# Hybrid GLA and MLA decoder block: the mixer residual kept token-major, its gates summed across partitions by GpSimd

## The chip, the cores and the metric

One Trainium2 chip, one core of it. The metric is the device time of one execution in microseconds (us). The kernel before takes 1746.09 us, the median of three runs (1744.71 to 1747.65).

## What is computed

One decoder block on 256 tokens of width 2048 in float32. A token mixer runs two branches (gated linear attention and latent attention), merges them, projects the merge by `w_out` and adds it to the residual under a gate; a SwiGLU FFN of width 5632 follows. Six modulation vectors of length 2048 come from one product of the conditioning vector with `ada_w`, of which each is a 2048 x 2048 block.

```python
mod = (c_act @ ada_w[l] + ada_b[l]).reshape(B, N_MOD, D)[:, :, None, :]
shift_m, scale_m, gate_m, shift_f, scale_f, gate_f = [mod[:, i] for i in range(N_MOD)]
...
x = x + gate_m * token_mix(h, ...)          # token_mix ends in merged @ w_out
h = rmsnorm(x, norm_ffn_g[l]) * (1.0 + scale_f) + shift_f
x = x + gate_f * swiglu(h, ffn_w_in[l], ffn_w_down[l])
return rmsnorm(x, final_norm_g)
```

## The kernel before

**Weights.** Every weight is used once, for all 256 tokens, and is streamed from HBM in *halves*: 256 rows by 512 columns, 512 KB, one DMA each on SyncE's queue (`load_raw`, L96). A half lands in a tile of a ring (`raw_tile`, L87): six tiles of the pool `raw`, and where `more_raw` (L92) has lent a big slot, four more, which the profile names `s`. A load can start when the tile that it takes over, ten loads back in the program, has been read. `split_raw` (L101) then makes two float32r parts of the half: ScalarE casts the high part `hi` (L107), VectorE subtracts for the low part `lo` (L108). Three buffers of each let the split run up to three halves ahead of TensorE.

**Products.** Three matmuls per product of a tile (high by high, high by low, low by high). `form_a` (L160) keeps 128 tokens of the activation stationary and streams 512 weight columns: the result is token-major, two PSUM banks for the two token tiles. `form_b` (L170) keeps 128 weight columns stationary and streams the 256 tokens: the result is feature-major. A half is 12 matmuls of 512 columns in `form_a` and 24 of 256 in `form_b`. A *group* is 512 output columns: 8 halves for a depth of 2048.

**Modulation in the background.** `ada_steps(m, c0)` (L243) computes 512 columns of modulation vector m, a *strip*: eight loads of 512 KB through the same ring, and for each load two multiply-adds of VectorE by c into the tile `ada` (L265, L267). For m < 5 the strip's 128 partial sums per column are then turned by four TensorE transposes (L289) and summed along the free axis by ScalarE (L291), which gives the vector feature-major in `mod`. The strips stand in a list `bg`; `tick()` (L154) is called once per weight half and lets `background()` (L118) take a step or none, by a rate `pace[0]`. A step is one `yield` of the generator. The strips of m = 2, 4 and 3 (mixer gate, FFN scale and shift), twelve in all, start with the attention stage and are spread over it and the three 2048 x 2048 projections (`mla_wo`, `gla_wo`, `w_out`). At the start of `w_out`'s last group, `background(1000)` (L838) issues all that is left before that group's first half.

**Around the output projection** (L832 to L866). x, which the prologue has stored feature-major in DRAM (`x_sp`, L428), is fetched back in four parts into `x1`. Four groups of `form_b` on `w_out` follow; after each, VectorE adds gate times result to x (L846; the gate is a column of `mod`). ScalarE squares x1 (L853), VectorE adds the squares of the sixteen blocks, a few matmuls with ones sum over partitions (L858), `rsqrt_mean` (L191) finds the reciprocal norms in a chain of small VectorE operations, `rows_of` (L208) spreads them by a matmul, and `modulate` (L317) makes the FFN's input. In the FFN's first loop, eight `turn_x1` (L895) transpose x1 back to token-major, where the final sum needs it.

The order of instructions on each engine is fixed when the program is built, by a scheduler that moves what isn't pinned with `keep_in_program_order`.

Of the kernel before, what the change touches and what calls it, by code (L numbers as in the profile page):

```python
# [17 lines left out]
D = 2048  # L18
S = 256
# [32 lines left out]
def tile_block(ctx: ExitStack, tc: tile.TileContext, x, positions, ada_w, ada_b, w_in, gla_gk_w, gla_wo,  # L52
# [18 lines left out]
    def k256(t):  # L71
        return t.rearrange("p (k t) -> p k t", t=S)
# [86 lines left out]

    def form_a(ps, w, ah, al, k0, first, last, cols):  # L160
        for kk, (hi, lo) in enumerate(w):
            k = k0 + kk
            for t in range(2):
                ts = slice(t * P, (t + 1) * P)
                st, en = first and kk == 0, last and kk == len(w) - 1
                T.matmul(ps[t][:, :cols], lhsT=ah[:, k, ts], rhs=hi, start=st, stop=False)  # L166
                T.matmul(ps[t][:, :cols], lhsT=ah[:, k, ts], rhs=lo, start=False, stop=False)  # L167
                T.matmul(ps[t][:, :cols], lhsT=al[:, k, ts], rhs=hi, start=False, stop=en)  # L168
# [22 lines left out]
    def rsqrt_mean(dst, ssq, n, w, eng=None):  # L191
        v, l = sb(w, "rv"), sb(w, "rl")
        V.tensor_scalar(out=v, in0=ssq, scalar1=1.0 / n, scalar2=EPS, op0=ALU.mult, op1=ALU.add)
        yi = dst.bitcast(I32)
        V.tensor_scalar(out=yi, in0=v.bitcast(I32), scalar1=1, scalar2=None, op0=ALU.logical_shift_right)
        V.tensor_scalar(out=yi, in0=yi, scalar1=-1.0, scalar2=float(0x5F3759DF), op0=ALU.mult, op1=ALU.add)
        for _ in range(3):
# [45 lines left out]
    def ada_steps(m, c0, cols=512, quick=None):  # L243
# [36 lines left out]
        if quick is not None:  # L280
# [4 lines left out]
            V.tensor_tensor(out=mod[:, cs], in0=ps[:, :nb], in1=cb[:, cs], op=ALU.add)  # L285
        elif m < 5:
            ps = aux_bank()
# [37 lines left out]

    x_sp = dram.tile([P, 4096], F32, name="x_sp")
    ga_sp = dram.tile([P, 4096], F32, name="ga_sp")
# [98 lines left out]
    for r in range(4):  # L426
        if r == 3:
            tc.keep_in_program_order(nc.sync.dma_start(out=x_sp, in_=xT))  # L428
            more_raw(slot(5))
# [209 lines left out]
    def gla_att(h):  # L639
# [66 lines left out]
        atts[h] = attv  # L706

    for b in range(4):
        bg += [ada_steps(m, 512 * b) for m in (2, 4, 3)]
    pace[0] = 0.2  # L710
# [122 lines left out]
    x1 = slot(4)  # L833
    x1k = k256(x1)
    pace[0] = 0.6
    for i in range(4):
        if i == 3:
            background(1000)  # L838
        for n, ps in enumerate(group(form_b, w_out, 512 * i, k256(mh), k256(ml), KT)):
            tick()  # L840
            if n == 3:
                cs = slice(1024 * i, 1024 * (i + 1))
                tc.keep_in_program_order(nc.sync.dma_start(out=x1[:, cs], in_=x_sp[:, cs]))
        for j in range(4):
            k = 4 * i + j
            V.scalar_tensor_tensor(out=x1k[:, k], in0=ps[j // 2][:, (j % 2) * S:(j % 2 + 1) * S],  # L846
                                   scalar=mod[:, 32 + k:33 + k], in1=x1k[:, k], op0=ALU.mult, op1=ALU.add)

    acc = sb(512, "w0")[:, :S]
    ps = aux_bank()  # L850
    for k in range(KT):
        q = acc if k == 0 else sb(S, "e", 3)
        A.activation(out=q, in_=x1k[:, k], func=AF.Square)  # L853
        if 0 < k < KT - 4:
            V.tensor_tensor(out=acc, in0=acc, in1=q, op=ALU.add)
        if k >= KT - 5:
            for t in range(2):
                T.matmul(ps[:, t:t + 1], lhsT=(acc if k == KT - 5 else q)[:, t * P:(t + 1) * P], rhs=ones[:, 0:1],  # L858
                         start=k == KT - 5 and t == 0, stop=k == KT - 1, skip_group_check=True)
    rc2 = sb(2, "rx")  # L860
    rsqrt_mean(rc2, ps[:, 0:2], D, 2)
# [32 lines left out]

    def turn_x1(k):  # L895
        tp = aux_bank()
        for t in range(2):
            for kk in range(2):
                T.transpose(out=tp[:, t * S + kk * P:t * S + (kk + 1) * P],
                            in_=x1k[:, k + kk, t * P:(t + 1) * P], identity=ident)  # L900
        A.copy(out=x1tv[:, :, k * P:(k + 2) * P], in_=tp.rearrange("p (t d) -> p t d", t=2))
        yield

    assert not ATT.busy()
    for ch in range(FFN // 512):
# [107 lines left out]
```

## Time and profile before

| what | us |
|---|---|
| three runs | 1747.65, 1744.71, 1746.09 (median 1746.09) |
| the profiled execution | 1749.17 |
| span of its records | 1747.1 |
| TensorE busy | 1705.2 (98%) |
| VectorE, ScalarE, GpSimd busy | 1226.6, 847.6, 99.7 (70%, 49%, 6%) |

The profile is of one further execution, 3.1 us above the median. The span is what its records cover; 2.1 us lie around it. Matmuls overlap in the pipeline, so a matmul's pace is read from the distance of starts, not from its duration. The chain that ended last runs through TensorE, in short pieces of the last product. `w_out` runs from about 878 to 985 us, the FFN from 993 us.

### The profile page before, as it was taken

Reading aid. Unit: us, or ns where it says so; the run is one execution under the profiler, and the core shown is the slowest. Engines: PE = TensorE matmul, PEld = TensorE weight load, DVE = VectorE, ACT = ScalarE, POOL = GpSimd, SP = SyncE. Lnnn points to the kernel's source line nnn. Section 1 sums busy time; section 2 is a strip of 40 time slices with the busy share of each in tenths; the row PEclk is TensorE's granted clock in tenths of the full one; section 3 lists DMA queues with packets and bytes.
Section 4 is the critical chain, followed back from the end, with each engine's and each line's share of the span. In section 5 each row is a group of like instructions: output and inputs, shape, how many; then the busy total and the mean of one; then the engine's idle time right before and its main releaser. Section 6 shows DMA issues by size and latency. Waiting matters only on the chain. (4 is left out here: it accounts for less than half of the span.)

```text
span 1747.1 us, 24089 instructions
## 1 busy us (share of the span) xinstructions
PE 1705.2 (98%) x8888; PEld 1461.1 (84%) x8888; DVE 1226.6 (70%) x1764; ACT 847.6 (49%) x1300; POOL 99.7 (6%) x136
## 2 busy tenths in 40 slices
PE   6999999999999999999999899999999999999997
PEld 5898899889999887788899888888888888788885
DVE  6899987587787477988887856666664444555556
ACT  4644445355766655544444444444444444444443
POOL 1370000000000001000000000000000000000001
PEclk8999999999999999999999899999999999999998
DMA  9999897655455498999998678778776666555652
GB/s 353 323 325 314 300 302 226 182 188 170 144 151 180 123 313 259 343 372 349 336 323 297 212 206 272 242 232 277 240 232 191 182 191 190 178 189 191 192 191 99
DMA packets 207349, 418.47 MB, mean 240 GB/s; under 512 B 12960, under 2 KB 31840, under 8 KB 206592
## 3 DMA queue, kind: packets, MB, share of 16 engines
q1 hardware_dynamic: 205472, 410.39, 72.1%
q0 software_dynamic: 1616, 6.49, 1.0%
q8 instruction: 69, 1.13, 0.3%
q14 instruction: 48, 0.39, 0.1%
q10 hardware_dynamic: 144, 0.07, 0.0%
HBM read 408.51 MB, written 8.39 MB: 239 GB/s over the span
## 5 line engine op out<-in xcount | busy, mean ns | idle before, releaser
L108 DVE TENSOR_TENSOR lo<-raw,hi 128x1024 fp32r<-128x1024 f32 (+3 forms) x524 | 600.9, 1152 | 396.9 <-ACT hi L107 394.4
L107 ACT CAST hi<-raw 128x1024 fp32r<-128x1024 f32 (+3 forms) x524 | 512.4, 984 | 620.6 <-PE mm L168 391.1
L167 PE MATMUL mm<-lo,s 128*128 128x512 f32 (+1 forms) x1520 | 598.4, 394 | 2.6 <-DVE lo L108 2.6
L168 PE MATMUL mm<-hi,s 128*128 128x512 f32 (+1 forms) x1520 | 590.4, 390 | 1.7 <-DVE s L322 1.7
L166 PE MATMUL mm<-hi,s 128*128 128x512 f32 (+1 forms) x1520 | 543.2, 393 | 4.3 <-ACT hi L107 2.1
L166 PEld LDWEIGHTS mm<-hi,s 128*128 128x128 f32 x1520 | 286.7, 190 | 63.3 <-ACT s L321 3.1
L167 PEld LDWEIGHTS mm<-lo,s 128*128 128x128 f32 x1520 | 287.8, 189 | 61.4 <-DVE lo L108 5.2
L168 PEld LDWEIGHTS mm<-hi,s 128*128 128x128 f32 x1520 | 287.3, 189 | 58.7 <-DVE s L322 2.0
L267 DVE SCALAR_TENSOR_TENSOR ada<-raw,cact,ada 128x512 f32<-128x512 f32 (+1 forms) x293 | 211.1, 724 | 10.5 <-DMA raw<-in_ada_w_dram 7.6
L176 PE MATMUL mm<-s,hi 128*128 128x256 f32 x672 | 191.7, 286 | 0.0
L177 PE MATMUL mm<-s,hi 128*128 128x256 f32 x672 | 190.1, 284 | 0.0
L178 PE MATMUL mm<-s,lo 128*128 128x256 f32 x672 | 188.3, 284 | 0.0
L107 ACT CAST hi<-s 128x1024 fp32r<-128x1024 f32 (+1 forms) x76 | 78.2, 1029 | 106.5 <-PE mm L168 46.2
L176 PEld LDWEIGHTS mm<-s,hi 128*128 128x128 f32 x672 | 128.7, 192 | 0.8 <-issue 0.3
L177 PEld LDWEIGHTS mm<-s,hi 128*128 128x128 f32 x672 | 128.8, 192 | 0.4
L178 PEld LDWEIGHTS mm<-s,lo 128*128 128x128 f32 x672 | 127.5, 192 | 0.0
L108 DVE TENSOR_TENSOR lo<-s,hi 128x1024 fp32r<-128x1024 f32 (+1 forms) x76 | 91.7, 1207 | 27.1 <-ACT hi L107 26.5
L926 PE MATMUL mm<-lo,w 128*128 128x512 f32 x160 | 62.7, 392 | 0.0
L927 PE MATMUL mm<-hi,w 128*128 128x512 f32 x160 | 62.4, 392 | 0.0
L267 DVE SCALAR_TENSOR_TENSOR ada<-s,cact,ada 128x512 f32<-128x512 f32 (+1 forms) x79 | 57.7, 730 | 0.5
L925 PE MATMUL mm<-hi,w 128*128 128x512 f32 x160 | 50.5, 394 | 0.7 <-ACT w L933 0.7
L451 DVE TENSOR_TENSOR s<-mm,s 128x512 f32<-128x512 f32 (+1 forms) x62 | 40.1, 672 | 0.2
(270 smaller groups left out, 1594.1 us busy)
## 6 DMA issues: line engine op xcount, KB each, us to landing
raw<-in_ffn_w_in_dram SPq DMA_DIRECT2D x176, 512.0 KB, 4.4
raw<-in_ada_w_dram SPq DMA_DIRECT2D x150, 512.0 KB, 4.9
raw<-in_w_in_dram SPq DMA_DIRECT2D x128, 512.0 KB, 4.7
raw<-in_ffn_w_down_dram SPq DMA_DIRECT2D x88, 512.0 KB, 4.4
s<-in_ada_w_dram SPq DMA_DIRECT2D x42, 512.0 KB, 5.9
s<-in_w_in_dram SPq DMA_DIRECT2D x32, 512.0 KB, 4.7
raw<-in_mla_wo_dram SPq DMA_DIRECT2D x20, 512.0 KB, 6.5
raw<-in_gla_wo_dram SPq DMA_DIRECT2D x20, 512.0 KB, 6.9
```

What stands on the lines that cost most here:

```text
L107: A.copy(out=hh_, in_=rr)
L108: V.tensor_tensor(out=ll_, in0=rr, in1=hh_.bitcast(F32), op=ALU.subtract)
L166: T.matmul(ps[t][:, :cols], lhsT=ah[:, k, ts], rhs=hi, start=st, stop=False)
L167: T.matmul(ps[t][:, :cols], lhsT=ah[:, k, ts], rhs=lo, start=False, stop=False)
L168: T.matmul(ps[t][:, :cols], lhsT=al[:, k, ts], rhs=hi, start=False, stop=en)
L176: T.matmul(o, lhsT=hi[:, pick], rhs=ah[:, k], start=st, stop=False, skip_group_check=True)
L177: T.matmul(o, lhsT=hi[:, pick], rhs=al[:, k], start=False, stop=False, skip_group_check=True)
L178: T.matmul(o, lhsT=lo[:, pick], rhs=ah[:, k], start=False, stop=en, skip_group_check=True)
L267: ins = V.scalar_tensor_tensor(out=acc, in0=raw[:, k - k0], scalar=c, in1=acc, op0=ALU.mult, op1=ALU.add)
L925: T.matmul(o, lhsT=ah[:, ts], rhs=hi[:, ns], start=first, stop=False)
L926: T.matmul(o, lhsT=ah[:, ts], rhs=lo[:, ns], start=False, stop=False)
L927: T.matmul(o, lhsT=al[:, ts], rhs=hi[:, ns], start=False, stop=last)
```

## The change

1. `w_out` goes by `form_a`, in 384 matmuls of 512 columns instead of 768 of 256. In the last group the last two halves are kept until both are split, and the first token tile is finished before the second.
2. x1 is token-major. x is read from its input in four parts, and `x_sp` is gone. The gate is needed along the free axis, on all partitions: `gm` (slot 3) receives the bias of the gate by a broadcast DMA, and the gate's sums come from DRAM (`gm_sp`) by four broadcast DMAs. VectorE multiplies, adds, and ScalarE squares with a row sum (`accum_out`).
3. For m = 2, 3, 4 GpSimd's `partition_all_reduce` sums the strip's accumulator over partitions, into a second buffer of the two-buffer tag `ada`; then comes one more `yield`. For m = 2 a DMA on SyncE's queue writes the sums to `gm_sp`; for m = 3 and 4 VectorE picks the diagonal of the four 128 x 128 blocks into `mod`.
4. The strips of m = 2 come first, then 4 and 3 by turns.
5. x1 is transposed to feature-major (`x1T`, slot 0) ahead of `modulate`, 32 transposes; the 32 of `turn_x1` in the FFN are gone.
6. `rsqrt_mean` has one operation less.

```diff
-    def form_a(ps, w, ah, al, k0, first, last, cols):
+    def form_a(ps, w, ah, al, k0, first, last, cols, rows=(0, 1)):
...
-            for t in range(2):
+            for t in rows:
...
-        V.tensor_scalar(out=yi, in0=v.bitcast(I32), scalar1=1, scalar2=None, op0=ALU.logical_shift_right)
-        V.tensor_scalar(out=yi, in0=yi, scalar1=-1.0, scalar2=float(0x5F3759DF), op0=ALU.mult, op1=ALU.add)
+        V.tensor_scalar(out=yi, in0=v.bitcast(I32), scalar1=-0.5, scalar2=float(0x5F3759DF), op0=ALU.mult, op1=ALU.add)
...
-        elif m < 5:
+        elif m in (2, 3, 4):
+            ar = sb(512, "ada", 2)
+            G.partition_all_reduce(ar, acc, channels=P, reduce_op=bass_isa.ReduceOp.add)
+            yield
+            if m == 2:
+                tc.keep_in_program_order(nc.sync.dma_start(out=gm_sp[:, c0:c0 + cols], in_=ar[0:1]))
+                return
+            for i in range(nb):
+                d = ar[:, i * P:(i + 1) * P]
+                V.tensor_tensor_reduce(out=d, in0=d, in1=ident, scale=1.0, scalar=0.0, op0=ALU.mult, op1=ALU.add,
+                                       accum_out=mod[:, b0 + i:b0 + i + 1])
+            V.tensor_tensor(out=mod[:, cs], in0=mod[:, cs], in1=cb[:, cs], op=ALU.add)
+        elif m < 2:
...
-            tc.keep_in_program_order(nc.sync.dma_start(out=x_sp, in_=xT))
...
+    bg += [ada_steps(2, 512 * b) for b in range(4)]
     for b in range(4):
-        bg += [ada_steps(m, 512 * b) for m in (2, 4, 3)]
+        bg += [ada_steps(m, 512 * b) for m in (4, 3)]
...
+    def gate_mix(i, n):
+        cs = slice(512 * i, 512 * (i + 1))
+        if n == 0 and i == 0:
+            tc.keep_in_program_order(nc.sync.dma_start(out=gm, in_=ada_b[:, 2 * D:3 * D].to_broadcast([P, D])))
+        elif n == 1:
+            gr = sb(512, "sc", 2)
+            tc.keep_in_program_order(nc.sync.dma_start(out=gr, in_=gm_sp[:, cs].to_broadcast([P, 512])))
+            tc.keep_in_program_order(V.tensor_tensor(out=gm[:, cs], in0=gm[:, cs], in1=gr, op=ALU.add))
+        elif n == 3:
+            tc.keep_in_program_order(nc.sync.dma_start(
+                out=x1v[:, :, cs], in_=x[0, :, cs].rearrange("(t p) c -> p t c", p=P)))
+
     for i in range(4):
         if i == 3:
             background(1000)
...
+        for n in range(KT // 2):
+            w = half(w_out, 2 * n, 512 * i, 512)
+            if i == 3 and n >= 6:
+                kept.append((2 * n, w))
+            else:
+                form_a(ps, w, k256(mh), k256(ml), 2 * n, n == 0, n == 7, 512)
             tick()
...
+        for t in range(2):
+            for k, w in kept:
+                form_a(ps, w, k256(mh), k256(ml), k, False, k == KT - 2, 512, (t,))
+            u = sb(512, "sc", 2)
+            j = 2 * i + t
+            V.tensor_tensor(out=u, in0=ps[t], in1=gm[:, cs], op=ALU.mult)
+            V.tensor_tensor(out=x1v[:, t, cs], in0=x1v[:, t, cs], in1=u, op=ALU.add)
+            A.activation(out=u, in_=x1v[:, t, cs], func=AF.Square, accum_out=sq[:, j:j + 1])
+            if j in (3, 5):
+                V.tensor_tensor(out=sq[:, j - 1:j + 1], in0=sq[:, j - 1:j + 1], in1=sq[:, j - 3:j - 1], op=ALU.add)
...
-        if 2 <= ch < 10:
-            ATT.wait.append(turn_x1(2 * (ch - 2)))
```

**SyncE's queue ahead of `w_out`'s last group.** L98 is a load into the ring, `s_6858` and `s_6818` the lent slot's tiles. Before (L843 fetches a part of x):

```order
L98 DMA s_6858<-in_ada_w_dram 128x2x512
L98 DMA raw<-in_w_out_dram 128x2x512
L98 DMA s_6858<-in_w_out_dram 128x2x512
L98 DMA s_6858<-in_ada_w_dram 128x2x512 x2
L98 DMA raw<-in_ada_w_dram 128x2x512 x3
L98 DMA raw<-in_w_out_dram 128x2x512 x3
L98 DMA s_6858<-in_w_out_dram 128x2x512 x2
```

Now (L856 fetches a quarter of the gate's sums); the first row here is the third group's last half, the last row the fourth group's first two:

```order
L98 DMA raw<-in_w_out_dram 128x2x512
L98 DMA s_6818<-in_ada_w_dram 128x2x512
L98 DMA raw<-in_ada_w_dram 128x2x512
L856 DMA sc<-gm_sp 128x512
L98 DMA raw<-in_ada_w_dram 128x2x512 x3
L98 DMA s_6818<-in_ada_w_dram 128x2x512
L98 DMA raw<-in_ada_w_dram 128x2x512
L98 DMA s_6818<-in_ada_w_dram 128x2x512 x2
L98 DMA raw<-in_ada_w_dram 128x2x512
L98 DMA s_6818<-in_ada_w_dram 128x2x512
L98 DMA raw<-in_ada_w_dram 128x2x512 x5
L98 DMA s_6818<-in_w_out_dram 128x2x512 x2
```

Five loads of `ada_w` stood together there; sixteen stand there now, between the 24th and the 25th half of `w_out`.

**VectorE at the end of `w_out`'s third group.** Before, L846 is the gated add of that group, which needs its last matmul; the two splits (L108) ahead of it are the fourth group's first two halves:

```order
L267 SCALAR_TENSOR_TENSOR ada<-s_6858,cact,ada 128x512 x2
L108 TENSOR_TENSOR lo<-raw,hi 128x1024 x2
L846 SCALAR_TENSOR_TENSOR s_8370<-mm,mod,s_8370 128x256 x4
L267 SCALAR_TENSOR_TENSOR ada<-s_6858,cact,ada 128x512
L108 TENSOR_TENSOR lo<-raw,hi 128x1024
L855 TENSOR_TENSOR w_9464<-w_9464,e 128x256
L267 SCALAR_TENSOR_TENSOR ada<-s_6858,cact,ada 128x512
L855 TENSOR_TENSOR w_9464<-w_9464,e 128x256
L108 TENSOR_TENSOR lo<-s_6858,hi 128x1024
```

Now L881 is the multiplication by the gate, L882 the addition to x1 (`s_8283`; `s_8284` is the gate), L885 adds row sums, L266 is the multiply-add of the strips; the first row splits the third group's last half, the last row the fourth group's first:

```order
L108 TENSOR_TENSOR lo<-raw,hi 128x1024
L264 TENSOR_SCALAR ada<-s_6818,cact 128x512
L266 SCALAR_TENSOR_TENSOR ada<-s_6818,cact,ada 128x512
L881 TENSOR_TENSOR sc<-mm,s_8284 128x512 x2
L882 TENSOR_TENSOR s_8283<-s_8283,sc 128x512 x2
L885 TENSOR_TENSOR sq<-sq 128x2
L266 SCALAR_TENSOR_TENSOR ada<-raw,cact,ada 128x512 x10
L266 SCALAR_TENSOR_TENSOR ada<-s_6818,cact,ada 128x512 x4
L108 TENSOR_TENSOR lo<-s_6818,hi 128x1024
```

Fourteen multiply-adds have come to stand between the third group's end and the fourth group's first split; no split of the fourth group stands ahead of L881.

**GpSimd between attention and the output gate**, now (L287 is the all-reduce with the change of GpSimd's program ahead of it, L604 a store of branch gates, L198 to L201 the reciprocal norms of one GLA head; none of L287 stood here before):

```order
L604 DMA ga_sp<-raw 128x1024
L672 MEMSET s_3630 128x512
L287 ISA
L287 ISA ada<-ada 128x512
L604 DMA ga_sp<-raw 128x1024 x2
L198 ISA
L198 TENSOR_TENSOR rl<-gr 128x2
L199 TENSOR_TENSOR rl<-rl,rv 128x2
L200 TENSOR_SCALAR rl<-rl 128x2
L201 TENSOR_TENSOR gr<-gr,rl 128x2
```

The all-reduce has been put in ahead of two stores, and a change of program before and after it; three more such changes to the all-reduce follow later in the queue.

## Rows read from the trace of the kernel before

**Rows 1.** The page: busy us of each engine, share of the span, instructions.

```profile
PE 1705.2 (98%) x8888; PEld 1461.1 (84%) x8888; DVE 1226.6 (70%) x1764; ACT 847.6 (49%) x1300; POOL 99.7 (6%) x136
```

**Rows 2.** Windows: us, TensorE, its weight loads, VectorE, ScalarE, GpSimd, granted clock, DMA share, GB/s.

```profile
960.50:984.90 24.40, 24.40 (x207) 24.40 (x205) 20.25 (x31) 11.30 (x22) 1.15 (x2) 1.00 0.77 268
993.00:999.15 6.15, 6.14 (x15) 4.79 (x15) 6.15 (x17) 4.20 (x9) 0.00 (x0) 0.50 0.00 0
```

**Rows 3.** Timeline of TensorE, `form_b` on `w_out`: start us, us, line, operation; 24 matmuls apart.

```profile
958.23 0.28 PE L176 MATMUL mm<-s,hi 128*128 128x256 f32 x1
...
961.11 0.28 PE L176 MATMUL mm<-s,hi 128*128 128x256 f32 x1
```

**Rows 4.** Timeline of TensorE, `form_a` on `gla_wo`, 12 matmuls apart.

```profile
829.83 0.39 PE L167 MATMUL mm<-lo,s 128*128 128x512 f32 x1
...
832.55 0.39 PE L167 MATMUL mm<-lo,s 128*128 128x512 f32 x1
```

**Rows 5.** TensorE's transposes: timeline around four, the source view of line 289.

```profile
981.38 0.28 PE L177 MATMUL mm<-s,hi 128*128 128x256 f32 x1
...
982.06 0.28 PE L176 MATMUL mm<-s,hi 128*128 128x256 f32 x1
L289 PE MATMUL aux<-ident,ada x48: 271/272/273, 555.3 to 981.8; 128*128 128x128 f32 x48
```

**Rows 6.** Timeline of SyncE's DMA queue: start us, us, line, DMA, count.

```profile
940.04 2.03 SPq L98 DMA_DIRECT2D s<-in_ada_w_dram  x2
943.18 4.18 SPq L98 DMA_DIRECT2D raw<-in_ada_w_dram  x3
948.69 3.25 SPq L98 DMA_DIRECT2D raw<-in_w_out_dram  x3
```

**Rows 7.** Waits of SyncE's queue: waiter and releaser, us in all, times, longest.

```profile
SPq L98 <- DVE lo L108: 850.5, 430, 9.3
```

**Rows 8.** Timeline of VectorE: two multiply-adds, a split, two multiply-adds.

```profile
972.50 1.53 DVE L267 SCALAR_TENSOR_TENSOR ada<-raw,cact,ada 128x512 f32<-128x512 f32 x2
973.95 1.22 DVE L108 TENSOR_TENSOR lo<-s,hi 128x1024 fp32r<-128x1024 f32 x1
975.08 1.53 DVE L267 SCALAR_TENSOR_TENSOR ada<-raw,cact,ada 128x512 f32<-128x512 f32 x2
```

**Rows 9.** Groups by line and shape: count, busy us, mean ns, idle before.

```profile
L451 DVE TENSOR_TENSOR s<-mm,s 128x512 f32<-128x512 f32 x58 | 38.1, 682 | 0.1
L564 DVE CUSTOM_DVE_ANT_0 sc<-aux,cft 128x128 f32<-128x128 f32 x16 | 4.6, 287 | 11.4 <-PE aux L560 11.4
L107 ACT CAST hi<-raw 128x1024 fp32r<-128x1024 f32 x459 | 482.5, 1052 | 601.4 <-PE mm L168 378.5 <-PE aux L927 60.4 <-PE mm L177 50.8
L976 ACT ACTIVATE sc<-s 128x512 f32<-128x512 f32 x8 | 5.0, 630 | 15.8 <-DVE s L974 12.8 <-DVE rl L205 2.1 <-DVE rv L193 0.9
L976 ACT ACTIVATION_READ_ACCUMULATOR sc<-s 128x1 f32 x8 | 1.5, 186 | 0.0
```

**Rows 10.** DMA issues: count, KB each, median us from issue to landing.

```profile
raw<-in_ffn_w_in_dram SPq DMA_DIRECT2D x176, 512.0 KB, 4.4
```

**Rows 11.** Timeline of TensorE and VectorE between the output projection and the FFN.

```profile
984.46 0.28 PE L178 MATMUL mm<-s,lo 128*128 128x256 f32 x1
...
993.01 0.79 PE L166 MATMUL mm<-hi,s 128*128 128x512 f32 x1 [1.18 <-ACT s L321]
993.60 0.63 PE L167 MATMUL mm<-lo,s 128*128 128x512 f32 x1
994.03 0.63 PE L166 MATMUL mm<-hi,s 128*128 128x512 f32 x1
...
987.65 0.16 DVE L193 TENSOR_SCALAR rv<-aux 128x2 f32<-128x2 f32 x1 [0.65 <-PE aux L858]
```

**Rows 12.** GpSimd: the group of line 300, and line 300 by source.

```profile
L300 POOL PARTITION_ALL_REDUCE w<-ada x4 | 14.8, 3702 | 294.3 <-DVE ada L267 294.3
L300 POOLq MODIFY_POOL_CONFIG  x2: 33/35/37, 976.6 to 976.6; - x2
```

More of the change, by code (lines that the diff above doesn't have):

```diff
@@ L323, in modulate @@
                                op0=ALU.add, op1=ALU.subtract)
-    x_sp = dram.tile([P, 4096], F32, name="x_sp")
+    gm_sp = dram.tile([1, D], F32, name="gm_sp")
     ga_sp = dram.tile([P, 4096], F32, name="ga_sp")
@@ L833, in tile_block @@
     x1 = slot(4)
-    x1k = k256(x1)
+    x1v = x1.rearrange("p (t d) -> p t d", t=2)
+    gm = slot(3)[:, :D]
+    sq = sb(8, "sq")
     pace[0] = 0.6
+    def gate_mix(i, n):
[9 more added lines that the diff above has]
+                out=x1v[:, :, cs], in_=x[0, :, cs].rearrange("(t p) c -> p t c", p=P)))
     for i in range(4):
@@ L838, in tile_block @@
             background(1000)
-        for n, ps in enumerate(group(form_b, w_out, 512 * i, k256(mh), k256(ml), KT)):
-            tick()
[L841 to L856, printed above, removed]
+        ps = [mm_bank(), mm_bank()]
+        cs = slice(512 * i, 512 * (i + 1))
+        kept = []
+        for n in range(KT // 2):
[4 more added lines that the diff above has]
+                form_a(ps, w, k256(mh), k256(ml), 2 * n, n == 0, n == 7, 512)
+            tick()
+            gate_mix(i, n)
@@ new lines, in tile_block @@
+        for t in range(2):
[8 more added lines that the diff above has]
+                V.tensor_tensor(out=sq[:, j - 1:j + 1], in0=sq[:, j - 1:j + 1], in1=sq[:, j - 3:j - 1], op=ALU.add)
+            elif j == 7:
+                V.tensor_tensor(out=sq[:, 6:8], in0=sq[:, 6:8], in1=sq[:, 4:6], op=ALU.add)
@@ L857, in tile_block @@
+    assert not ATT.busy()
+    rc2 = sb(2, "rx")
+    rsqrt_mean(rc2, sq[:, 6:8], D, 2)
+    x1T = slot(0)
+    x1k = k256(x1T)
+    for k in range(0, KT, 2):
+        ps = aux_bank()
+        for kk in range(2):
             for t in range(2):
[L858 to L861, printed above, removed]
+                T.transpose(out=ps[:, kk * S + t * P:kk * S + (t + 1) * P],
+                            in_=x1v[:, t, (k + kk) * P:(k + kk + 1) * P], identity=ident)
+        A.copy(out=x1T[:, k * S:(k + 2) * S], in_=ps)
@@ L865, in tile_block @@
         modulate(k, x1k, r2, 3, k256(fh), k256(fl))
-    x1t = slot(0)
     more_raw()
-    x1tv = x1t.rearrange("p (t d) -> p t d", t=2)
     acts = [slot(3), slot(2), None]
@@ L893, in turn_act @@
             yield
[L895 to L902, printed above, removed]
     assert not ATT.busy()
@@ L958, in tile_block @@
             held.append((ah, al, ws))
-    ot = slot(4)
+    ot = slot(0)
     otv = ot.rearrange("p (t d) -> p t d", t=2)
@@ L970, in tile_block @@
             ns = slice(n * 512, (n + 1) * 512)
-            d = x1tv[:, t, ns]
+            d = x1v[:, t, ns]
             u = sb(512, "ada", 2)
@@ L983, in tile_block @@
             if n < 2:
-                A.activation(out=otv[:, t, ns], in_=x1tv[:, t, ns], func=AF.Copy, scale=fr)
+                A.activation(out=otv[:, t, ns], in_=x1v[:, t, ns], func=AF.Copy, scale=fr)
             else:
-                V.scalar_tensor_tensor(out=otv[:, t, ns], in0=x1tv[:, t, ns], scalar=fr, in1=fg[:, ns],
+                V.scalar_tensor_tensor(out=otv[:, t, ns], in0=x1v[:, t, ns], scalar=fr, in1=fg[:, ns],
                                        op0=ALU.mult, op1=ALU.mult)
```

## The prediction

> **What bounds the kernel now.** Read the page first: TensorE is busy for 1705 us, 98% of the span [rows 1], and the chain of waits that ended last runs through it. So a change counts by what it takes from TensorE's queue, and by what it makes TensorE wait. The windows come next: in the output projection's last group TensorE and its weight loads are busy in every one of the 24.4 us, VectorE in 20.3 of them, and the DMA engines for 77% [rows 2]. Nothing there waits, but nothing has much room. Third, the waits of SyncE's queue: for 850 us it stood at a ring tile that VectorE had still to split [rows 7]. The ring is always full; what stands ahead in that queue delays what stands behind.
>
> **The sum, part by part.** It is made against the profiled execution's own 1749.2 us; the median of the runs shown is 3.1 lower, and the forecast is given against the median.
>
> *Form of the product.* A half in `form_b` takes 961.11 - 958.23 = 2.88 us [rows 3], in `form_a` 832.55 - 829.83 = 2.72 [rows 4]. The 24 halves of the first three groups give 24 x 0.16 = **-4.0**. The fourth group is walked through below.
>
> *Transposes of the strips.* From the matmul before four of them to the second one after it are 982.06 - 981.38 = 0.68 us, where two steps of 0.12 would be 0.24: four cost 0.44 [rows 5]. The trace has 48 from 555 us on, twelve strips, one of them in the fourth group: 11 x 0.44 = **-4.8**. On ScalarE the twelve sums go too, on VectorE 32 diagonals come (0.29 us each [rows 9], and a short read of the sum); neither engine sets the pace there, so I count nothing. Were VectorE's cover gone, the 32 would cost some 10 us.
>
> *Transposes of x1.* The FFN loses 32: 8 x 0.44 = **-3.5**. They come back in fours ahead of the FFN: sixteen in groups that TensorE bounds, **+1.8**; eight fall into the wait below, eight into the gap before the FFN.
>
> *The fourth group.* This is where I expect the loss. The extra `yield` takes a step of the background's budget for every strip without loading anything, so about ten loads fewer are done by the start of the last group, and `background(1000)` then issues the rest at once. The order shows it: sixteen strip loads in SyncE's queue ahead of that group's first half, where there were five. In the trace the five were issued between 940 and 947 us, the next half of `w_out` at 948.7 [rows 6], and TensorE never noticed, since two splits of the fourth group stood ahead of the third group's end. Now none does. Walk it from T, TensorE's last matmul of the third group:
> - VectorE: two multiplications and two additions of 0.68 [rows 9], then the row-sum addition waits for ScalarE's last square (0.63, its read 0.19 [rows 9]): T + 3.9.
> - Fourteen multiply-adds at (973.95 - 972.50) / 2 = 0.725 [rows 8]. The twelfth, at T + 12.6, frees the ring tile into which the fourth group's first half goes. It lands 4.4 us later [rows 10], ScalarE casts it in 1.05 [rows 9]: TensorE starts at about T + 18.2. The second half follows by 2.
> - The third half's tile is freed only by the next strip's second multiply-add. That stands behind both splits (975.08 - 973.95 = 1.13 each [rows 8]), four diagonals and the gate's addition: T + 24; with landing and cast, T + 29.3. TensorE has by then finished two halves and stands again.
> - From there VectorE has six splits and nine multiply-adds, 6 x 1.13 + 9 x 0.725 = 13.3: T + 42.6. The last matmuls come some 3.9 later, T + 46.5.
>
> The same stretch took 24.4 [rows 2]: **+22.1**. [...]
>
> *From the last matmul to the FFN.* Before, the norm's first operation starts 987.65 - 984.46 = 3.2 us after the last matmul's start, 2.9 after its end [rows 11]. Now the order puts two splits of the FFN's halves among the last products: a split that ends some 0.85 after TensorE, a multiplication, an addition, the second split, an addition, ScalarE's square and its read, the row-sum addition: 0.85 + 0.68 + 0.68 + 1.13 + 0.68 + 0.83 + 0.2 = 5.1, less 0.2 for the operation that `rsqrt_mean` lost: **+2.0**. That operation is also gone from the chains at start and end: **-0.4**.
>
> *GpSimd and SyncE.* An all-reduce takes 3.7 us [rows 12]; GpSimd idles, but four writes of the gate's sums now stand in SyncE's queue and hold it until the sums exist. Bounds: nothing, if the all-reduce is over when the queue arrives, and 4 x 3.7 = 14.8 if the queue is always there first. TensorE has up to three split halves, 8.2 us, as cover. I take **+2**, near the lower end. The trace shows a change of GpSimd's program only where the next all-reduce came 103 us later [rows 12], so its price stays open. [...]
>
> *At nothing:* the dropped store of x (TensorE was not waiting), and 2 MB more of broadcasts around the projection; the quarter of DMA time left over covers them [rows 2], and without it they would cost some 8 us at the 268 GB/s moved there.
>
> Sum: -4.0 - 4.8 - 3.5 + 1.8 + 22.1 + 2.0 - 0.4 + 2 = +15.2. From the profiled execution 1764.4, from the median **1761 us**.
>
> **Rivals.**
> - *Only VectorE's order costs, the loads don't.* If every half has landed when VectorE comes to it, the first split ends at T + 3.9 + 14 x 0.725 + 1.13 = T + 15.2, eight halves take 21.8, the half clock 2.4 more: T + 39.4, or +15.0 instead of +22.1. The rest without the +2 is -8.9: +6.1, **1752**. For it: loads of that size land in 4.4 at the median. Against: the tile is freed only by the twelfth multiply-add.
> - *SyncE's queue is held by GpSimd.* The four gate writes cost near 11 instead of 2: **1770**. For it: the queue's waits [rows 7] show no slack in the ring, and the writes were not there. Against: the program puts each some loads behind the end of its strip.
> - *Faster: TensorE's savings win.* If the wait at T is absorbed, the rest is -8.9: **1737**. It decides the sign as soon as the fourth group costs less than 8.9 more than before. For it: TensorE is the bound, and it loses 768 short matmuls and 48 transposes. Against: L881 needs the third group's last matmul, and the fourteen multiply-adds stand behind it; 10.2 us can't be hidden by a TensorE that has nothing split.
> - *Nothing measurable*: the wait and the savings cancel within 0.2% (3.5 us, about what a measurement of this kernel can tell from no change). It needs a fourth group of some 33 us, shorter than the walk of the first rival.
>
> **How the numbers follow.** The forecast 0.58, VectorE's order alone 0.17, SyncE's queue 0.12, faster 0.08, nothing measurable 0.05. Slower is 0.58 + 0.17 + 0.12 = 0.87. The forecast's own spread is some 6 us either way (landing times, the square, the +2), 1755 to 1767. The range reaches down past the first rival, to 1748, and up past the queue's, to 1774; it leaves out the faster case and the far end of the held queue.
>
> **What would show it.** Right: in the windows TensorE idles 15 to 19 us at one place, between the third and the fourth group, then again some 3 us; before the first matmul after it stand the fourteen multiply-adds on VectorE; the half of `w_out` behind the sixteen strip loads is issued after the third group's end. Steps of a `form_a` half in the first three groups are 2.72. No L289 after 555 us. The gap before the FFN is 10 to 11 us. Wrong: TensorE busy without a break across the fourth group, or idle time of several us at each of the first four all-reduces, or splits of the fourth group ahead of L881.

## The result, and the profile after

The changed kernel takes **1767.81 us** (median of four runs, 1766.34 to 1770.81), the kernel before beside it 1746.28 (four runs): a ratio of 1.0125, 95% interval 1.0112 to 1.0138. It is slower by 21.5 us; the forecast was 1761, slower by 15. The profiled execution took 1768.66, its span is 1766.9, 19.8 more than before.

The page's first part answers to [rows 1]:

```profile
PE 1698.3 (96%) x8436; PEld 1436.0 (81%) x8436; DVE 1242.8 (70%) x1811; ACT 836.3 (47%) x1204; POOL 148.9 (8%) x148
```

TensorE has 7 us less to do and the kernel takes 20 more: the loss is waiting. The windows say where (us, TensorE, its weight loads, VectorE, ScalarE, GpSimd, granted clock, DMA share, GB/s):

```profile
878.00:955.80 77.80, 77.78 (x356) 64.30 (x354) 66.93 (x93) 31.97 (x39) 6.76 (x2) 1.00 0.94 336
955.80:974.30 18.50, 1.28 (x8) 0.84 (x8) 12.51 (x19) 3.34 (x7) 3.23 (x1) 0.59 0.63 207
974.30:1006.75 32.45, 27.31 (x96) 20.26 (x96) 25.93 (x39) 9.44 (x9) 5.33 (x3) 0.87 0.74 267
1006.75:1018.25 11.50, 3.54 (x11) 1.94 (x10) 8.92 (x32) 4.21 (x9) 0.00 (x0) 0.65 0.55 168
1018.25:1023.55 5.30, 5.28 (x12) 4.14 (x13) 5.30 (x15) 3.20 (x7) 0.00 (x0) 0.50 0.00 0
```

T, the end of the third group of `w_out`, is 955.80. The second and third row are the fourth group: 50.95 us where [rows 2] had 24.4. The fourth row is the gap before the FFN, the fifth its restart at the lower clock. Set against the forecast:

| stretch | before | after | measured | forecast |
|---|---|---|---|---|
| start to the end of the third group | to 960.50 | to 955.80 | -4.7 | -5.0 |
| fourth group | 24.4 | 50.95 | **+26.6** | +22.1 |
| to the FFN's first matmul | 8.1 | 11.5 | +3.4 | +2.0 |
| FFN to the end | 754.1 | 748.6 | -5.5 | -3.9 |
| span | 1747.1 | 1766.9 | +19.8 | +15.2 |

VectorE from T on (timeline: start us, us, line, operation, idle before and what ended it):

```profile
955.14 1.37 DVE L881 TENSOR_TENSOR sc<-mm,s 128x512 f32<-128x512 f32 x2 [3.98 <-PE mm L168]
956.42 1.28 DVE L882 TENSOR_TENSOR s<-s,sc 128x512 f32<-128x512 f32 x2
958.51 0.16 DVE L885 TENSOR_TENSOR sq<-sq 128x2 f32<-128x2 f32 x1 [0.80 <-ACT sc L883]
958.59 7.83 DVE L266 SCALAR_TENSOR_TENSOR ada<-raw,cact,ada 128x512 f32<-128x512 f32 x10
966.46 3.12 DVE L266 SCALAR_TENSOR_TENSOR ada<-s,cact,ada 128x512 f32<-128x512 f32 x4
974.30 1.22 DVE L108 TENSOR_TENSOR lo<-s,hi 128x1024 fp32r<-128x1024 f32 x1 [4.73 <-ACT hi L107]
```

The fourteen multiply-adds stand between L881 and the first split, as the order had it. TensorE's breaks in that group, from its timeline:

```profile
974.32 1.22 PE L166 MATMUL mm<-hi,s 128*128 128x512 f32 x2 [15.68 <-ACT hi L107]
...
984.91 0.73 PE L166 MATMUL mm<-hi,s 128*128 128x512 f32 x2 [2.21 <-ACT hi L107]
...
1000.35 0.73 PE L166 MATMUL mm<-hi,s 128*128 128x512 f32 x2 [1.82 <-ACT hi L107]
```

The first two are the forecast's (T + 18.5 and T + 29.1; it said 18.2 and 29.3). The third is not. What led to it, from the timelines of ScalarE, SyncE's queue and GpSimd: first the cast of the group's first half, then the loads of the seventh and eighth, two broadcasts beside them, and their casts, which wait for the landing:

```profile
973.22 1.04 ACT L107 CAST hi<-s 128x1024 fp32r<-128x1024 f32 x1 [13.79 <-DMA s<-in_w_out_dram]
...
990.96 0.37 SPq L98 DMA_DIRECT2D raw<-in_w_out_dram  x1
...
992.78 0.37 SPq L98 DMA_DIRECT2D raw<-in_w_out_dram  x1
...
989.79 0.74 POOL L909 DMA_DIRECT2D s<-in_ada_b_dram  x1 [16.82 <-DMA raw<-in_w_out_dram]
990.54 0.54 POOL L910 DMA_DIRECT2D s<-in_final_norm_g_dram  x1
...
999.26 1.04 ACT L107 CAST hi<-raw 128x1024 fp32r<-128x1024 f32 x1 [6.48 <-DMA raw<-in_w_out_dram]
1000.56 1.05 ACT L107 CAST hi<-raw 128x1024 fp32r<-128x1024 f32 x1 [0.26 <-DMA raw<-in_w_out_dram]
```

From issue to the cast that starts with the landing are 8.3 us for the seventh half and 7.8 for the eighth, where the forecast had 4.4 for the landing. L909 and L910 bring 2 MB in the same moments. They are not new: the kernel before issues the same two at 975.5 and 976.1 us, 7 us after the last load of `w_out` was issued.

### The profile page after: what moved, and what is told of

Same layout as the page of the kernel before. It is cut to its first block, busy times and chain, and to the rows that moved or that the text cites. A ratio compares the mean times of both kernels' runs of the same rounds, so it can differ in the third digit from the quotient of the medians.

```text
span 1766.9 us, 23178 instructions
## 1 busy us (share of the span) xinstructions
PE 1698.3 (96%) x8436; PEld 1436.0 (81%) x8436; DVE 1242.8 (70%) x1811; ACT 836.3 (47%) x1204; POOL 148.9 (8%) x148
## 5 line engine op out<-in xcount | busy, mean ns | idle before, releaser
L108 DVE TENSOR_TENSOR lo<-raw,hi 128x1024 fp32r<-128x1024 f32 (+3 forms) x523 | 606.1, 1165 | 380.2 <-ACT hi L107 377.7
L167 PE MATMUL mm<-lo,s 128*128 128x512 f32 (+1 forms) x1648 | 648.1, 394 | 3.7 <-DVE lo L108 3.6
L168 PE MATMUL mm<-hi,s 128*128 128x512 f32 (+1 forms) x1648 | 641.7, 391 | 1.7 <-DVE s L333 1.7
L166 PE MATMUL mm<-hi,s 128*128 128x512 f32 (+1 forms) x1648 | 589.9, 394 | 25.6 <-ACT hi L107 23.8
L166 PEld LDWEIGHTS mm<-hi,s 128*128 128x128 f32 x1648 | 311.3, 190 | 91.4 <-ACT hi L107 25.9
L167 PEld LDWEIGHTS mm<-lo,s 128*128 128x128 f32 x1648 | 312.3, 190 | 69.2 <-DVE lo L108 7.6
L168 PEld LDWEIGHTS mm<-hi,s 128*128 128x128 f32 x1648 | 312.3, 190 | 63.9 <-DVE s L333 2.0
L266 DVE SCALAR_TENSOR_TENSOR ada<-raw,cact,ada 128x512 f32<-128x512 f32 (+1 forms) x294 | 213.2, 729 | 16.4 <-DMA raw<-in_ada_w_dram 13.3
L108 DVE TENSOR_TENSOR lo<-s,hi 128x1024 fp32r<-128x1024 f32 (+1 forms) x77 | 94.8, 1234 | 34.2 <-ACT hi L107 33.7
L176 PE MATMUL mm<-s,hi 128*128 128x256 f32 x416 | 118.8, 287 | 0.0
L177 PE MATMUL mm<-s,hi 128*128 128x256 f32 x416 | 117.7, 284 | 0.0
L178 PE MATMUL mm<-s,lo 128*128 128x256 f32 x416 | 116.2, 285 | 0.1
L176 PEld LDWEIGHTS mm<-s,hi 128*128 128x128 f32 x416 | 79.5, 191 | 0.8 <-issue 0.3
L177 PEld LDWEIGHTS mm<-s,hi 128*128 128x128 f32 x416 | 79.6, 191 | 0.4
L178 PEld LDWEIGHTS mm<-s,lo 128*128 128x128 f32 x416 | 78.6, 191 | 0.3 <-DVE lo L108 0.3
L287 POOL PARTITION_ALL_REDUCE ada<-ada x12 | 48.6, 4048 | 270.7 <-DVE ada L266 270.7
L266 DVE SCALAR_TENSOR_TENSOR ada<-s,cact,ada 128x512 f32<-128x512 f32 (+1 forms) x78 | 57.2, 733 | 0.8
```

The costliest lines, as they stand in the source:

```text
L108: V.tensor_tensor(out=ll_, in0=rr, in1=hh_.bitcast(F32), op=ALU.subtract)
L176: T.matmul(o, lhsT=hi[:, pick], rhs=ah[:, k], start=st, stop=False, skip_group_check=True)
L177: T.matmul(o, lhsT=hi[:, pick], rhs=al[:, k], start=False, stop=False, skip_group_check=True)
L178: T.matmul(o, lhsT=lo[:, pick], rhs=ah[:, k], start=False, stop=en, skip_group_check=True)
L266: ins = V.scalar_tensor_tensor(out=acc, in0=raw[:, k - k0], scalar=c, in1=acc, op0=ALU.mult, op1=ALU.add)
```

## The experiments

The theory is the forecast's: the background's extra step leaves strips undone, they are issued in one burst, and the last group waits behind them. Rivals: VectorE's order by itself, GpSimd's sums, slow landings of the loads.

**1. The extra step costs no load.** The step is paid back to the rate in the next call.

```diff
-            if next(bg[0], END) is END:
+            got = next(bg[0], END)
+            if got is END:
                 bg.pop(0)
             else:
                 n -= 1
+                pace[1] += got == "free"
...
             G.partition_all_reduce(ar, acc, channels=P, reduce_op=bass_isa.ReduceOp.add)
-            yield
+            yield "free"
```

> The changed kernel with one thing undone: the extra step of each strip no longer costs the background a load (the rate gets the step back in the next call). All-reduces, gates, token-major residual stay; the loads issued ahead of the last group of w_out fall from 16 to 5. Theory (the burst makes the wait): TensorE no longer idles 15.7 us at the start of the fourth group, the group from the third's last matmul to its own last one falls from 51 us to 22 to 26, and the time to 1738 to 1745. Rival 1 (VectorE's order with the token-major sums costs, the loads don't): idle of at least 8 us stays there, 1752 to 1760. Rival 2 (GpSimd's sums hold the queues): the time stays above 1760.

Measured: 1748.53, ratio 1.0007 (0.9998 to 1.0017). Windows of the last group and of the gap:

```profile
962.30:984.35 22.05, 22.05 (x102) 18.06 (x101) 19.76 (x24) 10.55 (x14) 4.08 (x3) 1.00 0.78 261
984.35:996.15 11.80, 3.32 (x11) 1.85 (x10) 9.29 (x32) 4.21 (x9) 1.25 (x1) 0.71 0.79 297
```

TensorE doesn't stand once in the last 22 us, and 19.3 us are back. Rivals 1 and 2 as stated fall: order and sums of the token-major residual are all still there. (The eleven loads took their 22 multiply-adds with them, so this run alone doesn't separate the loads from VectorE's work on them; the 13.8 us that the first cast waited for its load, above, do.) But 1738 to 1745 was missed by 3.5, and a kernel without the burst should have been near the 1737 of the forecast's faster rival.

**2. The burst alone.** The kernel before, with one empty step per strip.

```diff
         elif m < 5:
+            if m > 1:
+                yield
             ps = aux_bank()
```

> The kernel before with one thing added: each strip of m = 2, 3, 4 makes one empty step ahead of its transposes, so that the budget runs short there as in the changed kernel and 16 strip loads are issued at once ahead of the last group. Nothing of form_a, all-reduce or token-major x1 is in it. Theory: the burst alone makes TensorE stand 12 to 18 us at the start of the fourth group, and the time is 1760 to 1772. Rival (the wait belongs to the token-major sums): 1744 to 1750.

Measured: 1777.95, ratio 1.0177 (1.0162 to 1.0192), 31.4 slower than before. TensorE at the start of its fourth group:

```profile
971.41 1.12 PE L291 MATMUL aux<-ident,ada 128*128 128x128 f32 x4 [12.50 <-DVE ada L267]
...
976.59 0.58 PE L176 MATMUL mm<-s,hi 128*128 128x256 f32 x1 [4.07 <-ACT hi L107]
...
1002.55 0.38 PE L176 MATMUL mm<-s,hi 128*128 128x256 f32 x1 [2.59 <-ACT hi L107]
```

The first two make 16.6 us of waiting: for a strip's sums, whose transposes stand ahead of the group on TensorE, then for the first half's cast. They stand in a kernel that has no `form_a` in `w_out`, no all-reduce for these strips and no token-major x1. The burst is shown as the cause by adding it and by taking it away. The range, 1760 to 1772, was too low, as the forecast's 1761 was: here too the last halves came late (the third row). Why it costs 31.4 here and 19.3 in experiment 1 was not followed.

**3. GpSimd's broadcasts later.**

```diff
-    G.dma_start(out=gate_f, in_=ada_b[:, 5 * D:6 * D].to_broadcast([P, D]))
-    G.dma_start(out=fg, in_=final_norm_g.unsqueeze(0).to_broadcast([P, D]))
...
         if ch == 1:
+            tc.keep_in_program_order(nc.sync.dma_start(out=gate_f, in_=ada_b[:, 5 * D:6 * D].to_broadcast([P, D])))
+            tc.keep_in_program_order(nc.sync.dma_start(out=fg, in_=final_norm_g.unsqueeze(0).to_broadcast([P, D])))
```

> The changed kernel with GpSimd's two broadcasts of 2048 columns to 128 partitions (the FFN gate's bias and the final norm's weight, 1 MB each, issued at 989.8 and 990.5 us beside w_out's last loads) moved to the second chunk of the FFN, on SyncE's queue. Theory: the last two halves of w_out took 8.2 and 7.7 us to land in place of 4.4 because of these 2 MB; without them they land in 4 to 5.5, the wait of 1.8 us before the seventh half goes and the time falls by 3 to 5 us, to 1763 to 1765. Rival (the landing is slow for the burst's and the FFN's own loads): within 1.5 us of 1767.8, landing still over 7.

Measured: 1764.34, ratio 1.0096 (1.0081 to 1.0112), 3.5 below the changed kernel. The same two loads, and the eighth half's cast:

```profile
990.73 0.37 SPq L98 DMA_DIRECT2D raw<-in_w_out_dram  x1
...
991.94 0.37 SPq L98 DMA_DIRECT2D raw<-in_w_out_dram  x1
...
996.07 1.05 ACT L107 CAST hi<-raw 128x1024 fp32r<-128x1024 f32 x1 [0.55 <-DMA raw<-in_w_out_dram]
```

4.1 us from issue to cast in place of 7.8, and the break ahead of the seventh half is gone. The group takes 47.8 us in place of 50.95: that is most of the 4.5 that the forecast missed.

**4. The strips of m = 3 and 4 back on TensorE.** Experiment 1 with, for these eight strips, the old branch (four transposes, four sums by ScalarE, no extra step) in place of the all-reduce and the diagonals.

```diff
-        elif m in (2, 3, 4):
+        elif m == 2:
...
-        elif m < 2:
+        elif m < 5:
             ps = aux_bank()
```

> e1_step_given_back with the eight strips of m = 3 and 4 again turned by four TensorE transposes and summed by ScalarE, without all-reduce and without the extra step; the four gate strips keep the all-reduce. Theory: 8 x 0.44 = 3.5 us more on TensorE than e1_step_given_back, less what waits for loads hide: slower than it by 1.5 to 4. Rival (GpSimd's part costs on the path, as the forecast's +2 had it): same time as e1_step_given_back or faster.

Measured: 1742.71, ratio 0.9977 (0.9967 to 0.9987): 5.8 *faster* than experiment 1. The theory is wrong, its rival right: the all-reduces with their diagonals cost more than the transposes that they replace. The profiled executions are only 3.6 us apart (that of experiment 1 is the fastest of its ten). 2.0 of these are the gap, 9.8 us here in place of 11.8:

```profile
982.50:992.30 9.80, 5.80 (x39) 4.02 (x37) 7.14 (x24) 7.96 (x23) 0.00 (x0) 1.00 0.93 358
```

In experiment 1 the last strip's all-reduce runs ahead of the gap, and VectorE's split beside it takes 2.53 us and ends with it; the gate's products stand behind that split, and four diagonals of the strip between them and x1 (GpSimd's timeline, then VectorE's):

```profile
981.54 4.05 POOL L289 PARTITION_ALL_REDUCE ada<-ada  x1 [1.06 <-DVE ada L268]
...
983.15 2.53 DVE L108 TENSOR_TENSOR lo<-raw,hi 128x1024 fp32r<-128x1024 f32 x1 [0.65 <-ACT hi L107]
985.60 1.27 DVE L883 TENSOR_TENSOR sc<-mm,s 128x512 f32<-128x512 f32 x2
986.80 0.28 DVE L296 CUSTOM_DVE_ANT_0 ada<-ada,ident 128x128 f32<-128x128 f32 x1
...
987.65 0.68 DVE L884 TENSOR_TENSOR s<-s,sc 128x512 f32<-128x512 f32 x1
```

In experiment 4 that split takes 1.23. So the split loses 1.3 us and the diagonals 0.85. The forecast had set the 32 diagonals at nothing, for want of a place where VectorE sets the pace; this is one. `w_out` also ends 1.9 us earlier in experiment 4 (982.50 against 984.35); what makes that difference was not followed.

**5. The gate's writes on GpSimd's queue.** The changed kernel, with the four DMAs of the sums issued by GpSimd.

```diff
-                tc.keep_in_program_order(nc.sync.dma_start(out=gm_sp[:, c0:c0 + cols], in_=ar[0:1]))
+                G.dma_start(out=gm_sp[:, c0:c0 + cols], in_=ar[0:1])
```

> The changed kernel with the four writes of the gate's sums issued by GpSimd, right behind its own all-reduce, in place of SyncE's queue, where the last two of them waited 2.3 and 2.7 us for the sums. Theory (the burst and its landing make the loss; no TensorE wait follows these holds directly): within 1.5 us of 1767.8. Rival (SyncE's queue held by GpSimd costs TensorE time, as the forecast's +2 had it): 2 to 5 us faster, 1763 to 1766, and the wait of 2.3 us at 716 us gone.

Measured: 1768.56, ratio 1.0129 (1.0111 to 1.0148): no change, and the waits of SyncE's queue for the sums, 5.0 us in the changed kernel, are gone. The held queue costs nothing that can be measured; the forecast's +2 for it and its second rival fall.

**6. The same in experiment 4.** The same line moved.

```diff
-            tc.keep_in_program_order(nc.sync.dma_start(out=gm_sp[:, c0:c0 + cols], in_=ar[0:1]))
+            G.dma_start(out=gm_sp[:, c0:c0 + cols], in_=ar[0:1])
```

> e4_back_strips_on_tensore with the same move of the gate's writes to GpSimd. There SyncE stood 3.5 us at the fourth write (719.2 to 722.6 us), and TensorE waited 1.6 and 2.4 us at 721 and 733, each with a restart at the lower clock. Theory (these waits come from the held queue): they go, 2 to 5 us faster than e4, 1738 to 1741. Rival (between 720 and 950 us the DMA engines are busy for 93 to 103 percent, so a load issued sooner lands no sooner): within 1 us of 1742.7, the waits only move.

Measured: 1743.32, ratio 0.9979 (0.9969 to 0.9988), within 1 us of experiment 4. The waits at 721 and 733 us stayed, 4.5 us together, although the hold was gone, as the rival has it; the DMA share in this run is 0.94 to 1.02 from 720 to 950 us.

**7. More strips in the attention stage.** Experiment 6 with three rates changed.

```diff
-    pace[0] = 0.2
+    pace[0] = 0.35
...
-    pace[0] = 0.8
+    pace[0] = 0.65
...
-    pace[0] = 0.65
+    pace[0] = 0.6
```

> e6 with the background's rates changed: 0.35 in place of 0.2 in the attention stage, where the DMA engines are busy for about half, then 0.65 for 0.8 and 0.6 for 0.65 in the two projections. Of the strips' loads 103 in place of 95 are issued ahead of mla_wo; the last group's burst is 3. Theory (the DMA-bound stretch from 720 to 950 us swallows what TensorE saves there): 2 to 6 us faster than e6. Rival (TensorE is the bound there and the savings are real): within 1 us of e6, or slower because VectorE's work in the attention stage gets in the way.

Measured: **1734.79**, ratio 0.9932 (0.9915 to 0.9949): 8.5 below experiment 6, more than the theory's 2 to 6, and faster than both kernels. The windows of 715 to 775 us, in experiment 6:

```profile
715.00:775.00 60.00, 55.02 (x233) 43.79 (x232) 52.03 (x64) 28.41 (x37) 3.96 (x2) 0.97 0.97 357
```

and here:

```profile
715.00:775.00 60.00, 60.00 (x272) 49.57 (x271) 52.57 (x66) 31.04 (x47) 2.10 (x6) 1.00 1.02 375
```

The DMA share is 0.97 there and 1.02 here; with eight loads fewer to bring from there to `w_out`, TensorE no longer stands. Not all of the gain lies here: `w_out` ends 6.9 us earlier than in experiment 6 (975.85 against 982.75), the gap is 0.6 shorter, and the FFN's first 5 us run at a granted clock of 1.00 with 21 matmuls, where experiment 4 has 0.66 and 15: six steps of 0.227, an estimated 1.4 more.

**8. The same rates in the kernel before.** The same three lines.

```diff
-    pace[0] = 0.2
+    pace[0] = 0.35
...
-    pace[0] = 0.8
+    pace[0] = 0.65
...
-    pace[0] = 0.65
+    pace[0] = 0.6
```

> The kernel before with the rates of e7 alone (0.35, 0.65, 0.6, 0.6): 103 strip loads ahead of mla_wo in place of 95, 3 in front of the last group in place of 5. Theory (the rates give back only what a TensorE that had become faster lost while it waited for loads; before, TensorE stood 0.3 us between 720 and 950 us, so there is nothing to give back): 1744 to 1748. Rival (the rates are a gain of their own, and the change has no part in e7's): 1736 to 1740.

Measured: 1749.33, ratio 1.0017 (1.0008 to 1.0027): slower by 2.8, past the theory's end and away from the rival's; where the 2.8 go was not followed. The rates are no gain of their own: the 8.5 us come only together with the change (in experiment 6's form).

**9. The change as it is, with rates alone.**

```diff
-    pace[0] = 0.2
+    pace[0] = 0.4
...
-    pace[0] = 0.8
+    pace[0] = 0.75
...
-    pace[0] = 0.6
+    pace[0] = 0.7
```

> The changed kernel as it is, all-reduces, extra step, SyncE's gate writes and all, with four rates changed: 0.4, 0.75, 0.65 and 0.7 in the attention stage and the three projections, so that the budget that the extra steps take is paid: 102 loads ahead of mla_wo in place of 92, 3 in front of the last group in place of 16. Theory (the burst and the missing supply in the DMA-bound stretch are the whole loss, and the rest of the change is a gain, 3.5 us of transposes more than in e7): no wait above 1.5 us between 720 us and the norm, 1730 to 1738. Rival (GpSimd's sums cost on the path, as e1 stood 6 us above e4): 1739 to 1745.

Measured: 1757.00, ratio 1.0061 (1.0045 to 1.0078). The wait behind the burst is gone, and another has come, in the list of TensorE's waits the longest:

```profile
PE gx L762 <- DVE s L753: 13.6, 1, 13.6
```

L753 needs a GLA head's norm, which GpSimd computes. GpSimd's timeline:

```profile
719.13 1.04 POOL L200 TENSOR_SCALAR rl<-rl 128x2 f32<-128x2 f32 x1
729.41 3.25 POOL L287 PARTITION_ALL_REDUCE ada<-ada  x1 [9.24 <-issue]
739.71 0.18 POOL L201 TENSOR_TENSOR gr<-gr,rl 128x2 f32<-128x2 f32 x1 [7.05 <-issue]
```

The scheduler has put an all-reduce between the last two operations of the norm. It takes 3.25 us. GpSimd stands 9.2 us ahead of it and 7.1 behind it without waiting for another engine; the records of its changes of program (MODIFY_POOL_CONFIG, at 720.4 and 732.6 us) stand at the start of both stretches, 9.0 us ahead of the all-reduce and 7.1 ahead of the norm's last operation.

**10. Rates under which the order is clear.** No all-reduce stands inside a head's norm here.

```diff
-    pace[0] = 0.2
+    pace[0] = 0.45
...
-    pace[0] = 0.8
+    pace[0] = 0.75
...
-    pace[0] = 0.6
+    pace[0] = 0.75
```

> The changed kernel with other rates than e9 (0.45, 0.75, 0.65, 0.75): 104 strip loads ahead of mla_wo, none left for the last group, and with these no all-reduce stands between the operations of one head's norm on GpSimd, as it did in e9, where GpSimd's two changes of program took 9.0 and 7.1 us and TensorE stood 13.6 us for that head. Theory (those 13.6 us and their restart are e9's whole excess, and what is left of the change is a gain): no wait of TensorE above 3 us between 600 us and the norm, 1733 to 1742. Rival (the all-reduces of m = 3 and 4 cost wherever they stand): 1750 or more, with TensorE waits of 5 us and more behind GpSimd.

Measured: 1747.93, ratio 1.0011 (1.0002 to 1.0021). The 13.6 us are gone, but a wait of 5.6 has come for a split, which VectorE's timeline has behind this row:

```profile
632.49 0.49 DVE L264 TENSOR_SCALAR ada<-raw,cact 128x512 f32<-128x512 f32 x1 [9.39 <-POOL ada L287]
```

and GpSimd's this:

```profile
629.21 3.25 POOL L287 PARTITION_ALL_REDUCE ada<-ada  x1 [5.78 <-issue]
```

The all-reduce's result takes the second buffer of the tag `ada`, and the next strip needs the first, which the all-reduce has still to read; the all-reduce starts 5.8 us after the norm, and the profile names no other engine for that wait (`<-issue`). Neither theory nor rival: better than 1750, worse than 1742. What else stands between this and experiment 7, 13 us away, was not followed.

## Why the prediction was right, and where its sizes were off

- *The fourth group, +22.1.* Right in place, cause and order of events; too small by 4.5. The walk holds to 0.3 us as far as the third half (T + 18.5, T + 29.1). The step that failed is "from there VectorE has six splits and nine multiply-adds": VectorE's work was not the last thing there, the loads were. The casts of the seventh and eighth half waited for their landing, until T + 43.5 and T + 44.8; TensorE could start on the two at T + 44.6 and ended at T + 51 in place of 46.5. The walk used the median landing of 4.4 for all halves, where the last two took 8.2 and 7.7 us; in the kernel before, the eight loads of that group already took 3.7 to 7.3. Experiment 3 measured what the two broadcasts of L909 and L910 cost beside these loads, 3.5 us. The forecast did not look at them (the 2 MB that it set at nothing are others, the gate's bias and sums): in the kernel before they came when that group's loads had landed, now they run beside the last two.
- *The form of the product, -4.0.* In `w_out`'s third group twelve matmuls now take 2.72 us from start to start, the step that the forecast read from `gla_wo`:

```profile
950.18 0.62 PE L166 MATMUL mm<-hi,s 128*128 128x512 f32 x2
...
952.90 0.62 PE L166 MATMUL mm<-hi,s 128*128 128x512 f32 x2
```

- *Strips' transposes, -4.8, and GpSimd with SyncE, +2.* Up to T the sum agrees (-4.7 for -5.0), but that is partly luck, for one of its terms is wrong. The +2 stood for SyncE's queue, and that is worth nothing (experiment 5). TensorE lost time elsewhere, 2.0 and 0.5 us at 718, where it came for a half that had not landed; why it was late was not followed. What experiment 4 shows is the balance for the eight strips of m = 3 and 4: without the burst the all-reduces and diagonals lose 5.8 us against the transposes.
- *The gap, +2.0.* Measured +3.4. The chain had VectorE's two splits, but nothing of the last strip. Its all-reduce runs at the end of the group; the second of two splits beside it takes 3.27 us in place of 1.22 and ends with it, and the strip's four diagonals follow. The first token tile's product, which the chain took as done by then, starts only 0.6 us after TensorE's last matmul (VectorE, then GpSimd):

```profile
1002.14 4.40 DVE L108 TENSOR_TENSOR lo<-raw,hi 128x1024 fp32r<-128x1024 f32 x2
1006.49 0.29 DVE L294 CUSTOM_DVE_ANT_0 ada<-ada,ident 128x128 f32<-128x128 f32 x1
...
1007.34 0.69 DVE L881 TENSOR_TENSOR sc<-mm,s 128x512 f32<-128x512 f32 x1
...
1002.40 4.05 POOL L287 PARTITION_ALL_REDUCE ada<-ada  x1 [11.33 <-DVE ada L266]
```

- *x1's transposes and the shorter norm, -3.9.* Measured -5.5. Some of the rest is the restart at the lower clock, 5.3 us here and 6.15 before [rows 2]; the remainder was not traced.
- *The rivals.* Only VectorE's order: against it stands that ScalarE's first cast of the group, at 973.22, waited 13.8 us for the load, and experiment 2, which has another order there and a like wait. The 2.4 that this rival adds for the half clock, twelve matmuls at the step of [rows 11], can be read in the changed kernel: behind the 15.7 us the granted clock is 0.50 from 974.30 to 979.55, and twelve matmuls take 5.5 us from start to start (974.32 to 979.81) in place of 2.72. SyncE's queue: experiment 5; no run shows a far end of the held queue, only the 5.0 us of waits that went there at no gain. Nothing measurable: it needed a fourth group of some 33 us, and that took 50.95. Faster, 1737: it did not happen. Three things keep it away, the burst (31.4 us where experiment 2 adds it, 19.3 where experiment 1 takes it away), the all-reduces and diagonals of m = 3 and 4 (5.8), and the old rates of the background (8.5), under which TensorE waits in the stretch where the DMA share is 0.97; without them experiment 7 stands at 1734.79. That this lies near 1737 is partly luck: experiment 7 has the transposes of eight strips back, 8 x 0.44 = 3.5 us that the rival counts as saved, and rates that it did not have.

What the forecast did not see as a whole is the last of the three. It booked TensorE's savings in full where TensorE was the bound by a hair; the windows of the kernel before show TensorE busy and a DMA share of 1.02 and 0.94 beside it:

```profile
715.00:775.00 60.00, 59.39 (x268) 48.42 (x267) 52.76 (x70) 30.54 (x46) 2.32 (x12) 1.00 1.02 379
775.00:950.00 175.00, 175.00 (x1029) 155.26 (x1028) 149.98 (x191) 80.65 (x123) 0.00 (x0) 1.00 0.94 330
```

[rows 2] showed this only for the last group, where the share is 0.77.

## What to carry to other kernels

A background stream with a budget pays for every step that it is given, also for an empty one, and what it doesn't get done falls due at the next point that drains it: count the loads left at that point before and after an edit, on the queue that they share with the work in front. A faster engine can lose its gain to waits in a stretch in which another resource is nearly full, as TensorE did in experiment 6 from 715 to 775 us, busy for 55.0 of 60 beside DMA engines at 0.97; move the other's work out of the stretch along with the edit (here three rates), and test the same move in the kernel before to know whose gain it is. An all-reduce on an idle engine was not free here: with that engine's other small jobs on TensorE's path it cost a wait of 13.6 us (experiment 9), and VectorE's splits beside it took up to 3.27 us in place of 1.22.

## What was not expected of the hardware

- **GpSimd around an all-reduce.** In experiment 9 GpSimd stood 9.2 us ahead of an all-reduce of 3.25 and 7.1 behind it, with the record of a change of its program at the start of each stretch; in experiment 10 it stood 5.8 ahead of another of 3.25.
- **VectorE beside an all-reduce.** In the changed kernel, at nine of the strips' twelve all-reduces a split of VectorE beside it took 1.30 to 3.27 us in place of 1.22, and ended within 0.1 us of the all-reduce's end. At two others, at 509 and 822 us, splits beside it kept 1.22; what tells the cases apart was not tried.
- **Landing under broadcasts.** Two 512 KB loads took 8.2 and 7.7 us to land while two 1 MB broadcasts ran on another queue. From issue to cast they took 8.3 and 7.8, and 3.7 and 4.1 without the broadcasts (experiment 3).
- **A gap filled with transposes kept the full clock once, and once not.** In experiment 7 all 32 transposes of x1 fall into the gap before the FFN, and TensorE stands for at most 1.4 us between them. Windows of that gap and of the FFN's first 5 us:

```profile
975.85:985.05 9.20, 5.13 (x35) 3.59 (x33) 7.03 (x23) 6.79 (x15) 0.00 (x0) 1.00 0.54 186
985.05:990.00 4.95, 4.92 (x21) 4.05 (x22) 4.95 (x14) 3.35 (x7) 0.00 (x0) 1.00 0.00 0
```

The same two stretches before, where TensorE stood 3.0 us at a time:

```profile
984.60:993.00 8.40, 3.65 (x24) 2.76 (x22) 5.59 (x20) 2.53 (x6) 0.00 (x0) 0.76 0.76 295
993.00:998.00 5.00, 4.99 (x12) 3.93 (x13) 5.00 (x14) 3.12 (x8) 0.00 (x0) 0.50 0.00 0
```

At a granted clock of 1.00, 21 matmuls fit where 12 did at 0.50. The 8.4 us before are not without matmuls: some twenty small ones stand in them. But transposes and short waits don't decide it: in experiment 4 the gap of 9.8 us holds the same 32 transposes and four of the last strip, TensorE stands for at most 1.3 us between them, and the FFN's first 5 us still begin at the lower clock:

```profile
992.30:997.30 5.00, 5.00 (x15) 3.97 (x16) 5.00 (x14) 2.99 (x7) 0.00 (x0) 0.66 0.03 10
```

What makes the difference was not found.
